# v of four pairs computed at once and kept in memory, and six merge gates moved into the pairs of a three-branch decoder layer

## The chip, the cores and the metric

The kernel runs on one core of a Trainium2 chip. The metric is the device time of one execution in microseconds. Before the change it is 1905.27 us, the median of three runs (1904.55 to 1906.85).

## What is computed

One layer on a sequence of S = 1024 rows of width D = 1024, all in float32. The input is normalised to h, and one projection of h with 14 blocks of columns feeds three branches; a convolution with a layer norm (a), a gated linear recurrence over 8 heads of 128 (b), and attention with a forget gate over 16 heads of 64 (c). Each branch is multiplied by its own gate, projected, weighted by a merge gate and summed; the sum is projected once more and added to the input. Cut to what matters here:

```python
h = rms_norm(x, g)
p = h @ w_in                              # columns: a: val, glu, gate; b: q, f, i, gate; c: q, k, v, gate, f; merge
out_b = hgrn2(silu(q), f, i, lb, g)       # v = i: scores @ v, state += k^T v, per head of 128
logits = q @ k.T / 8 + F[:, None] - F[None, :]   # c: F = cumsum(log_sigmoid(f))
out_c = softmax(causal(logits)) @ v
y = sum(sigmoid(merge[b]) * ((branch[b] * silu(gate[b])) @ w_branch[b]) for b in "abc")
out = x + y @ w_out
```

For `scores @ v` both branches need v with the sequence in the partitions: 8 blocks of 128 rows by 128 columns for each head of b, and the same for each two heads of c.

## The kernel before

**Projections.** A job is a product of 128 columns of a weight matrix with the whole sequence. Each float32 factor is split into a high and a low part (`whi`, `wlo` by `split` at L342, ScalarE casts, VectorE subtracts; `hT_hi`, `hT_lo` for h), and three products are added up: hi by hi, hi by lo, lo by hi. So a job is 2 halves (512 columns of the sequence each) of 8 x 3 = 24 matmuls of 128x512, with the weights stationary. The result has the projected columns in the partitions and the sequence in the free dimension. Three of the eight PSUM banks take turns for these jobs (`ps_lin`, L224); the other five are for the attention and the recurrence.

**Order of the jobs.** `lin` (L359) goes through the list `jobs` that is built from L1141 on. First stands the narrow job of the forget gate of c (`fgate_done`, L411, with a scan over the sequence and 8 small transposes in `fgate2`, L435). Then come 8 pairs; a pair c holds q, k, v, gate of two heads of branch c (`col(7)` to `col(10)`) and q, f, v, gate of one head of branch b (`col(3)` to `col(6)`), 8 jobs in all. After the pairs stand the convolution's jobs, the branch projections of c and b (`bjob`) with the merge gates of c, b, then the gate of a (`ag`), the eight merge gates of a (`mjob("a", j)`), the eight projections of a and the output.

**v.** The two v jobs of a pair write v into a tile `vT` (columns in the partitions); `vprep` (L549) then turns it with 8 transposes of 128x128 on TensorE into two PSUM banks, and ScalarE copies these into the tile `V`. The attention (`att`, L579) or the recurrence (`hgrn`, L711) of the pair starts at the end of this.

**What sets the order of the work.** While the program is written, a planner (`Sched`, L86) runs `lin` and the coroutines of attention, recurrence and convolution side by side, by its own estimates of each engine's time, and so decides how their instructions are mixed. 18 work tiles of 128x1024 (`F`, class `Free`, names fa0 to fa9 and fb0 to fb7) go round among all of them. Each engine then executes its instructions in the order in which they are written, and a wait holds up all that stands behind it on its engine. All DMAs are issued from one queue, SP's, in order too. The fb tiles are given up after the last pair (`swap`, L1157), and the branch inputs `yhi`, `ylo` take their memory; `yload` (L960) then reads the first of them.

**The end of the pairs.** The recurrence of a head ends with a partition all-reduce on GpSimd, a logarithm and an exponential with a table load each on ScalarE, a product on VectorE, and a store into `yb`.

Of the kernel before, what the change touches and what calls it, by code (L numbers as in the profile page):

```python
# [39 lines left out]
ORD = "01ab"  # L40
AHB = 2
# [8 lines left out]
class Free:  # L50
# [148 lines left out]
def build(tc, x, norm_g, w_in, conv_w, conv_b, ln_g, ln_b, hgrn_g, f_bias, qn_g, kn_g,  # L199
# [93 lines left out]
    mdram = dram.tile([KT, P, S], F32, name="mdram")  # L293

# [42 lines left out]

    def fetch(j):
# [20 lines left out]
    def lin(jobs, hooks):  # L359
        seq = [(0, 0), (1, 0), (2, 0), (0, 1), (1, 1), (2, 1)]  # L360
        seq += [(n, h) for n in range(3, len(jobs)) for h in (0, 1)]
        for m, (n, half) in enumerate(seq):
            j = jobs[n]
            for i in {3: (3,), 5: (4,)}.get(m, (n + 2,) if n > 2 and not half else ()):
                if i < len(jobs):
                    fetch(jobs[i])
            for i in {5: (3,)}.get(m, (n + 1,) if n > 2 and not half else ()):
                if i < len(jobs):
                    split(jobs[i])
# [166 lines left out]
    def v_pre(st):  # L536
        def f():
            yield need(2 + RES)
            st["vT"], st["V"] = F.get(), F.get()
        return f  # L540

    def v_done(st, tag, cb):
        def f(half, hs, ps):
            sc.act(st["vT"][:, hs], ps, AF.Copy)
            if half == 1:
                sc.start(vprep(st, tag, cb), f"v{tag}{st['c']}")
        return f

    def vprep(st, tag, cb):  # L549
        vT, V = st["vT"], st["V"]  # L550
        yield
        pss = yield from bget(2)
# [4 lines left out]
        bput(*pss)  # L557
        yield
        fput(vT)
        st["v"] = True  # L560
        if cb is not None:
            cb()

    def g_pre(st):
        def f():
            yield need(1 + RES)
            st["gt"] = F.get()
# [417 lines left out]
    def br_pre(b, j):  # L985
        def f():
            if b != "c":
# [150 lines left out]
    def col(o, c, w=P):  # L1138
# [4 lines left out]
                    narrow=True))  # L1143
    t128 = [const.tile([P, KT], F32, name=f"t128_{i}") for i in range(2)]
    for c in range(KT):
# [4 lines left out]
        jobs.append(Job(col(9, c), hX, v_done(sa, "c", (lambda s: lambda: sc.start(att(s), f"att{s['c']}"))(sa)), v_pre(sa)))  # L1150
        jobs.append(Job(col(10, c), hX, g_done(sa), g_pre(sa)))
        jobs.append(Job(col(3, c), hX, bq_done(sb), bq_pre(sb)))
        jobs.append(Job(col(4, c), hX, bf_done(sb), bf_pre(sb)))
# [192 lines left out]
```

## Time and profile before

| | before |
|---|---|
| median of three runs | 1905.27 us (1904.55 to 1906.85) |
| profiled execution, its own time | 1904.65 us |
| span of its trace | 1902.9 us |
| TensorE busy | 1885.2 us, 99% |
| VectorE busy | 1285.2 us, 68% |
| ScalarE busy | 953.6 us, 50% |
| GpSimd busy | 186.2 us, 10% |
| DMA moved | 140.82 MB, mean 74 GB/s |

The busy shares are means over unlike stages. In the pairs (about 55 to 1000 us) ScalarE is busy 74% of the time and VectorE 68%; in the stage of the convolution (1110 to 1450 us) VectorE is busy 96%, ScalarE 17%; in the last stage (from 1548 us) both are mostly idle. TensorE has next to no gap in any of them, at a granted clock of 1.00 but for one stretch in the first 40 us. The durations of single matmuls overlap (0.39 us each, 0.23 us from start to start), so lengths of time on TensorE are read from starts.

### The profile page before, as it was taken

To read this page: it belongs to the slowest core of one execution; us is meant where nothing else is said; L and a number is where in the kernel's file an instruction comes from. 1 tells how busy PE (TensorE), PEld (TensorE's weight loads), DVE (VectorE), ACT (ScalarE), POOL (GpSimd) and SP (SyncE) were. 2 spreads that over 40 slices of the span, in tenths; PEclk is the share of its full clock that TensorE was granted. 3 is DMA by queue.
4 is the path that set the end of the run, shared out by engine and by line. 5 is a ranking of instruction groups with operands and counts; after the bars stand their busy time and mean duration, and the time that the engine had idled before them with its cause. 6 is when DMAs were issued, how large, how long until landed. Compare 5 with 4: busy or idle time off the path is not lost.

```text
span 1902.9 us, 27032 instructions
## 1 busy us (share of the span) xinstructions
PE 1885.2 (99%) x11075; PEld 1548.8 (81%) x11075; DVE 1285.2 (68%) x1692; ACT 953.6 (50%) x1508; POOL 186.2 (10%) x164
## 2 busy tenths in 40 slices
PE   8999999999999999999999999999999999999999
PEld 6877878878878788787887888888888888888888
DVE  6567595775856857659577999999995467413431
ACT  6777768767687687776875411111221234321210
POOL 2021120211202111112021100000000010000000
PEclk9999999999999999999999999999999999999999
DMA  4111101111111111110111322222444553213431
GB/s 147 48 31 45 56 23 45 56 45 45 34 45 45 34 52 38 45 56 23 45 56 46 133 78 67 78 67 67 134 147 151 194 160 92 85 45 104 118 129 49
DMA packets 173011, 140.82 MB, mean 74 GB/s; under 512 B 4909, under 2 KB 155445, under 8 KB 172888
## 3 DMA queue, kind: packets, MB, share of 16 engines
q1 hardware_dynamic: 172888, 139.10, 23.7%
q8 instruction: 86, 1.41, 0.3%
q14 instruction: 37, 0.30, 0.1%
HBM read 109.72 MB, written 29.36 MB: 73 GB/s over the span
## 4 chain that ended last, share of the span: by engine, by line
PE 85%; ACT 7%; DVE 3%; DMA 3%; issue 1%; SPq 0%; POOL 0%; DVEq 0%; ACTq 0%; POOLq 0%
PE bank L111 84%; ACT fb L124 4%; ACT khi L124 1%; DVE fa L128 1%; PE bank L115 1%; ACT L124 1%; DMA zdram<-fa 1%; ACT fa L124 1%; DVE fb L128 1%; DMA fa<-zdram 1%; DMA fb<-in_hgrn_norm_g_dram 1%; DMA wraw<-in_w_in_dram 0%; ACT whi L354 0%; DVE klo L132 0%; DVE wlo L355 0%
## 5 line engine op out<-in xcount | busy, mean ns | idle before, releaser
L111 PE MATMUL bank<-hT_hi,whi 128*128 128x512 f32 x1792 | 706.8, 394 | 0.0
L111 PE MATMUL bank<-hT_hi,wlo 128*128 128x512 f32 x1792 | 701.3, 391 | 0.8 <-DVE wlo L355 0.8
L111 PE MATMUL bank<-hT_lo,whi 128*128 128x512 f32 x1792 | 701.2, 391 | 0.0
L111 PEld LDWEIGHTS bank<-hT_hi,wlo 128*128 128x128 f32 x1792 | 336.8, 188 | 72.9 <-issue 2.4
L111 PEld LDWEIGHTS bank<-hT_hi,whi 128*128 128x128 f32 x1792 | 337.0, 188 | 69.8 <-issue 3.2
L111 PEld LDWEIGHTS bank<-hT_lo,whi 128*128 128x128 f32 x1792 | 337.3, 188 | 63.8 <-issue 0.2
L354 ACT ACTIVATE whi<-wraw 128x1024 fp32r<-128x1024 f32 x137 | 144.9, 1058 | 356.9 <-PE bank L111 346.9
L132 DVE SCALAR_TENSOR_TENSOR fa<-fa,taps,fa 128x1024 f32<-128x1024 f32 x240 | 300.0, 1304 | 0.4
L355 DVE TENSOR_TENSOR wlo<-wraw,whi 128x1024 fp32r<-128x1024 f32 x137 | 191.8, 1400 | 112.2 <-ACT whi L354 109.9
L128 DVE TENSOR_TENSOR fa<-fa,fa 128x512 f32<-128x512 f32 (+3 forms) x226 | 173.8, 784 | 67.0 <-ACT fa L124 50.4
L124 ACT ACTIVATE fa<-bank 128x512 f32<-128x512 f32 (+2 forms) x182 | 102.5, 572 | 141.7 <-PE bank L111 131.0
L111 PE MATMUL bank<-yhi,whi 128*128 128x512 f32 x384 | 149.4, 389 | 0.0
L111 PE MATMUL bank<-yhi,wlo 128*128 128x512 f32 x384 | 149.2, 389 | 0.0
L111 PE MATMUL bank<-ylo,whi 128*128 128x512 f32 x384 | 149.2, 389 | 0.0
L124 ACT ACTIVATE fb<-bank 128x512 f32<-128x512 f32 (+5 forms) x262 | 114.2, 451 | 40.6 <-PE bank L111 32.1
L128 DVE TENSOR_TENSOR fa<-fa,fb 128x512 f32<-128x512 f32 (+1 forms) x121 | 81.8, 676 | 59.0 <-ACT fb L124 37.8
L124 ACT ACTIVATE fb<-bank,negF,rk 128x256 f32<-128x256 f32 (+1 forms) x184 | 89.2, 549 | 47.7 <-PE bank L111 31.8
L124 ACT ACT_TABLE_LOAD x83 | 106.5, 1283 | 4.5 <-DVE fb L128 3.0
L132 DVE SCALAR_TENSOR_TENSOR fa<-fa,bank 128x512 f32<-128x512 f32 x96 | 65.7, 686 | 60.0 <-PE bank L111 60.0
L124 ACT ACTIVATE fa<-fa 128x256 f32<-128x256 f32 (+3 forms) x109 | 75.9, 721 | 55.3 <-DMA zdram<-fa 29.6
L124 ACT ACTIVATE fb<-fb 128x1024 f32<-128x1024 f32 (+2 forms) x96 | 88.1, 953 | 15.8 <-DVE fb L128 14.8
L111 PEld LDWEIGHTS bank<-yhi,wlo 128*128 128x128 f32 x384 | 72.1, 188 | 15.0
(163 smaller groups left out, 2128.7 us busy)
## 6 DMA issues: line engine op xcount, KB each, us to landing
wraw<-in_w_in_dram SPq DMA_DIRECT2D x113, 512.0 KB, 3.8
wraw<-in_w_branch_dram SPq DMA_DIRECT2D x24, 512.0 KB, 3.9
zdram<-fa SPq DMA_DIRECT2D x16, 512.0 KB, 4.1
mdram<-fa SPq DMA_DIRECT2D x32, 256.0 KB, 2.0
fa<-mdram SPq DMA_DIRECT2D x16, 512.0 KB, 3.8
fa<-zdram SPq DMA_DIRECT2D x16, 512.0 KB, 3.3
fa<-in_x_dram SPq DMA_DIRECT2D x9, 512.0 KB, 5.2
yc<-fb SPq DMA_DIRECT2D x8, 512.0 KB, 2.6
```

What stands on the lines that cost most here:

```text
L111: self.nc.tensor.matmul(out, lhsT=lhsT, rhs=rhs, start=start, stop=stop)
L115: self.nc.tensor.transpose(out, in_, ident)
L124: return self.nc.scalar.activation(out, in_, func, **kw)
L128: self.nc.vector.tensor_tensor(out=out, in0=a, in1=b, op=op)
L132: self.nc.vector.scalar_tensor_tensor(out=out, in0=a, scalar=s, in1=b, op0=op0, op1=op1)
L354: pin(nc.scalar.activation(j.hi, j.raw, AF.Copy))
L355: pin(eng.tensor_tensor(out=j.lo, in0=j.raw, in1=j.hi.bitcast(F32), op=ALU.subtract))
```

## The change

For v, four pairs are done at once. A `VJob` takes 512 columns of v's weights (four pairs of one branch). Its weights stay in 8 of the work tiles, four for the high and four for the low parts (`vfetch`), and now slices of hT of 128 rows are stationary and the weights move: 8 groups of 24 matmuls of 128x512, each with a result of 128 rows of the sequence by 512 columns of v (`vgroup`). The result is copied to a work tile and stored to DRAM (`vdram`); `g_pre` of each pair reads the pair's 128 columns back into `V`. `vprep` with its transposes and copies is gone. The number of 128x512 matmuls is the same: 4 x 192 instead of 16 x 48. All four VJobs stand in pair 0: after k, after the gate of c, after q of b and after f of b.

The six merge gates of a with j = 2 to 7 are no longer computed after `ag`, but one each in pairs 1 to 6, behind the gate of c (`pjob`). Their tanh is stored to `gdram` and read back in `br_pre`. What each engine gets more or less, counted in the instructions of both kernels: TensorE 128 transposes less; ScalarE 32 copies of 128x512 less and 10 table loads more (84 to 94); VectorE as many as before; 60 more DMAs on SP's queue. In TensorE's order the kind of matmul changes (projection to something else or back) 327 times instead of 295.

The core of the diff:

```diff
+EARLY = [("a", j) for j in range(2, 8)]
...
+    vdram = {(t, h): dram.tile([4, P, S], F32, name=f"v{t}{h}") for t in "cb" for h in range(2)}
+    gdram = {(b, j): dram.tile([P, S], F32, name=f"g{b}{j}") for b, j in EARLY}
...
+    def vfetch(j):
+        yield need(KT + 2)
+        j.lo = [F.get(dt=F32R, w=S) for _ in range(4)]
+        j.hi = [F.get(dt=F32R, w=S) for _ in range(4)]
+        for n, (lo, hi) in enumerate(zip(j.lo, j.hi)):
+            raw = F.get()
+            nc.sync.dma_start(out=raw[:, 0:S].rearrange("p (k c) -> p k c", k=2),
+                              in_=j.src[n * 256:(n + 1) * 256].rearrange("(k p) c -> p k c", p=P))
+            with tc.high_priority(HP):
+                nc.scalar.activation(hi[:, 0:S], raw[:, 0:S], AF.Copy)
+                nc.vector.tensor_tensor(out=lo[:, 0:S], in0=raw[:, 0:S],
+                                        in1=hi[:, 0:S].bitcast(F32), op=ALU.subtract)
+            fput(raw)
...
+    def vgroup(j):
+        w = lambda ts, k: ts[k // 2][:, k % 2 * H2:(k % 2 + 1) * H2]
+        for i in range(KT):
...
+            ps = ps_lin()
+            for k in range(KT):
+                hh, hl = (h[:, k, i * P:(i + 1) * P] for h in hT)
+                sc.mm(ps, hh, w(j.hi, k), k == 0, False, 228)
+                sc.mm(ps, hh, w(j.lo, k), False, False, 228)
+                sc.mm(ps, hl, w(j.hi, k), False, k == KT - 1, 228)
...
+            sc.act(ot[:, i % 2 * H2:(i % 2 + 1) * H2], ps, AF.Copy)
+            if i % 2:
+                for n in range(2):
+                    nc.sync.dma_start(
+                        out=vdram[j.tag, j.half][:, :, (i - 1 + n) * P:(i + n) * P].rearrange("c p e -> p c e"),
+                        in_=ot[:, n * H2:(n + 1) * H2].rearrange("p (c e) -> p c e", c=4))
...
-    def vprep(st, tag, cb):
...
-        for k in range(KT):
-            sc.tr(pss[k // 4][:, k % 4 * P:(k % 4 + 1) * P], vT[:, k * P:(k + 1) * P], ident)
-        for half in range(2):
-            sc.act(V[:, half * H2:(half + 1) * H2], pss[half], AF.Copy)
...
-    def g_pre(st):
+    def g_pre(st, tag, cb):
...
+            nc.sync.dma_start(out=st["V"][:, 0:S], in_=vdram[tag, c // 4][c % 4])
...
+            if (b, j) in gdram:
+                yield need(1, True)
+                mg[b, j] = F.get(True)
+                nc.sync.dma_start(out=mg[b, j][:, 0:S], in_=gdram[b, j])
...
+        if c == 0:
+            jobs.append(VJob(col(9, 0, 4 * P), "c", 0))
...
+        elif early:
+            jobs += [pjob(*bj) for bj in early[:1]]
...
-    jobs += [mjob("a", j) for j in range(KT)]
+    jobs += [mjob("a", j) for j in range(KT) if ("a", j) not in gdram]
```

**VectorE at the start.** The rows of x are normalised one block of 128 after the other (`fa4`, `fa5`, the last are fa6 and fa7) and go to TensorE to be turned into hT; `vecs` is a table of small vectors that comes from TensorE. Before:

```order
L1246 TENSOR_SCALAR fa4_5_149<-fa4_5_149,ss_120 128x1024 [waits DMAHW6_49,DVE_49]
L1234 TENSOR_SCALAR ss_120<-ss_120 128x1 [waits Activation_49]
L1242 RECIPROCAL ss_120<-ss_120 128x1
L1243 SCALAR_TENSOR_TENSOR ss_120<-ss_120 128x1 [waits DVE_49]
L1244 TENSOR_SCALAR ss_120<-ss_120 128x1 [waits DVE_49]
L1246 TENSOR_SCALAR fa5_6_150<-fa5_6_150,ss_120 128x1024 [waits DMAHW5_49,DVE_49]
```

With the change, where `fb0_19` is the low part of the first weights of v:

```order
L1311 TENSOR_SCALAR fa4_5_159<-fa4_5_159,ss_120 128x1024 [waits DMAHW6_49,DVE_49]
L1299 TENSOR_SCALAR ss_120<-ss_120 128x1 [waits Activation_49]
L359 TENSOR_TENSOR fb0_19_549<-fa2_27_557,fa8_23_553 128x1024 [waits DMAHW3_49,DMAHW2_49,DMAHW4_49,DMAHW1_49,DMAHW6_49,DMAHW0_49,PE_49]
L1307 RECIPROCAL ss_120<-ss_120 128x1
L1361 COPY vecs_110<-bank7_83 128x280
L129 TENSOR_TENSOR fb4_13_370<-fb4_13_370,fb5_14_371 16x512 [waits Activation_49]
L1308 SCALAR_TENSOR_TENSOR ss_120<-ss_120 128x1 [waits DVE_49]
L1362 TENSOR_SCALAR taps_111<-vecs_110 128x248 [waits DVE_49]
...
L1311 TENSOR_SCALAR fa5_6_160<-fa5_6_160,ss_120 128x1024 [waits DMAHW5_49,DVE_49]
```

The subtraction for v's weights, which waits for TensorE, stands ahead of the normalisation of fa5 and of the two that follow.

**TensorE behind k of pair 0.** `fb1_18` is the result of the forget gate's scan; its transposes are the 128x16 rows. Before, the v job of pair 0 (`whi_541`, `wlo_542`) fills the time up to them, 45 matmuls of 128x512 (from the first row here to the last but one):

```order
L111 MATMUL bank0_76<-hT_hi_143,whi_541 128x512 [waits Activation_49]
L111 MATMUL bank0_76<-hT_lo_144,whi_541 128x512
L115 MATMUL bank4_80<-ident_84,fb3_17_417 128x128 x2
L111 MATMUL bank1_77<-hT_hi_143,whi_541 128x512 [waits Activation_49]
L111 MATMUL bank0_76<-hT_hi_143,wlo_542 128x512 [waits DVE_49]
...
L111 MATMUL bank1_77<-hT_hi_143,wlo_542 128x512
L115 MATMUL bank3_79<-ident_84,fb1_18_506 128x16 [waits DVE_49]
```

With the change, where fa8, fa9, fa0, fa1 hold the high parts and fb0, fb4, fb5, fb2 the low parts of the first VJob's weights:

```order
L112 MATMUL bank0_76<-fa8_23_553,hT_hi_153 128x512 [waits Activation_49]
L112 MATMUL bank0_76<-fb0_19_549,hT_hi_153 128x512
...
L112 MATMUL bank1_77<-fa9_24_554,hT_hi_153 128x512
L116 MATMUL bank4_80<-ident_84,fb3_17_427 128x128 x4
L116 MATMUL bank3_79<-ident_84,fb1_18_514 128x16 [waits DVE_49]
L116 MATMUL bank3_79<-ident_84,fb1_18_514 128x16 x7
L112 MATMUL bank0_76<-fb4_20_550,hT_hi_153 128x512 [waits DVE_49]
```

There are 14 matmuls of the VJob ahead of the transposes that wait for the scan, and the next ones need fb4_20. That tile takes the place of the scan's input, as VectorE's order shows (`fb4_13` and `fb5_14` are the scan's inputs):

```order
L483 MEMSET fb5_14_371 16x1024 [waits DVE_49]
L133 SCALAR_TENSOR_TENSOR klo0_131<-bank2_78,gk_115,khi0_129 64x512 [waits Activation_49]
L485 SCALAR_TENSOR_TENSOR fb1_18_514<-fb5_14_371,fb4_13_370 16x1024 [waits DVE_49]
L359 TENSOR_TENSOR fb4_20_550<-fa3_28_561,fa9_24_554 128x1024 [waits DMAHW7_49,DVE_49]
L359 TENSOR_TENSOR fb5_21_551<-fa4_29_565,fa0_25_555 128x1024 [waits DMAHW2_49]
```

**VectorE at the end of pair 7.** `fa1_277` before and `fb7_332` after is the tile of the last head's result, `fa4_294` and `fa3_351` the factor that the exponential gives, `ylo0` the first input of the branch projection of c; the rows with `taps` are the convolution. Before:

```order
L132 SCALAR_TENSOR_TENSOR fa8_298_8801<-fa6_297_8800,taps_111,fa8_298_8801 128x1024
L128 TENSOR_TENSOR fa1_277_8304<-fa1_277_8304,fa4_294_8655 128x1024
L132 SCALAR_TENSOR_TENSOR fa0_301_9155<-fa9_300_9154,taps_111,fa0_301_9155 128x1024
L132 SCALAR_TENSOR_TENSOR fa8_298_8801<-fa6_297_8800,taps_111,fa8_298_8801 128x1024
L128 TENSOR_TENSOR ylo0_9121<-ylo0_9121,yhi0_9113 128x1024
L128 TENSOR_TENSOR ylo1_9122<-ylo1_9122,yhi1_9114 128x1024
```

With the change:

```order
L129 TENSOR_TENSOR fb7_332_8610<-fb7_332_8610,fa3_351_9073 128x1024 [waits Activation_49]
L133 SCALAR_TENSOR_TENSOR fa1_355_9404<-fa8_354_9403,taps_111,fa1_355_9404 128x1024 [waits DVE_49] x5
L129 TENSOR_TENSOR ylo0_9370<-ylo0_9370,yhi0_9362 128x1024 [waits DMAHW3_49,DMAHW5_49,DMAHW2_49,Activation_49]
L133 SCALAR_TENSOR_TENSOR fa1_355_9404<-fa8_354_9403,taps_111,fa1_355_9404 128x1024 [waits DVE_49]
L129 TENSOR_TENSOR ylo1_9371<-ylo1_9371,yhi1_9363 128x1024 [waits DMAHW4_49,Activation_49]
L133 SCALAR_TENSOR_TENSOR fa1_355_9404<-fa8_354_9403,taps_111,fa1_355_9404 128x1024 [waits DVE_49]
L129 TENSOR_TENSOR ylo2_9372<-ylo2_9372,yhi2_9364 128x1024 [waits DMAHW5_49,Activation_49]
L406 TENSOR_TENSOR wlo_9710<-wraw_9635,whi_9709 128x1024 [waits DMAHW7_49,PE_49,Activation_49]
```

The last result now stands in an fb tile, whose memory goes to `yhi` and `ylo`. On TensorE 223 rows lay between the last matmul of the last head and the first of the branch projection of c, nearly all of them 128x512; now there are 72, all of them 128x512:

```order
L112 MATMUL bank7_83<-fa9_350_9072,fa2_349_9071 128x128 [waits DVE_49]
L112 MATMUL bank1_77<-hT_hi_153,whi_9637 128x512 [waits Activation_49]
...
L112 MATMUL bank2_78<-hT_hi_153,whi_9573 128x512 [waits Activation_49]
...
L112 MATMUL bank0_76<-hT_hi_153,whi_9637 128x512 [waits Activation_49]
...
L112 MATMUL bank2_78<-yhi0_9362,whi_9709 128x512 [waits DMAHW2_49,DMAHW1_49,DMAHW5_49,DVE_49,DMAHW7_49,Activation_49,Pool_49]
L112 MATMUL bank2_78<-ylo0_9370,whi_9709 128x512 [waits DVE_49]
L112 MATMUL bank2_78<-yhi0_9362,wlo_9710 128x512 [waits DVE_49]
```

The second of the three jobs' halves waits for ScalarE to empty bank2 into a tile (`fa3_357`) that takes the place of `fa3_351`, the factor above.

## Rows read from the trace of the kernel before

**Rows 1.** Page: busy time of TensorE; the convolution's group on VectorE (busy, mean ns, idle).

```profile
PE 1885.2 (99%) x11075; PEld 1548.8 (81%) x11075; DVE 1285.2 (68%) x1692; ACT 953.6 (50%) x1508; POOL 186.2 (10%) x164
...
L132 DVE SCALAR_TENSOR_TENSOR fa<-fa,taps,fa 128x1024 f32<-128x1024 f32 x240 | 300.0, 1304 | 0.4
```

**Rows 2.** Waits of TensorE: line, releaser, us in total, times, longest.

```profile
PE bank L111 <- ACT fa L124: 1.8, 7, 0.3
...
PE bank L111 <- DVE wlo L355: 0.8, 1, 0.8
```

**Rows 3.** Windows: length, busy us of PE, PEld, DVE, ACT, POOL; clock, DMA.

```profile
247.70:371.40 123.70, 123.17 (x883) 99.91 (x881) 84.49 (x133) 92.07 (x156) 20.01 (x15) 1.00 0.15 43
...
120.00:125.00 5.00, 4.34 (x38) 2.61 (x37) 5.00 (x10) 4.99 (x7) 0.00 (x0) 1.00 0.00 0
```

**Rows 4.** Timeline of TensorE: start, us, engine, line, operation, count.

```profile
59.40 0.39 PE L111 MATMUL bank<-hT_lo,whi 128*128 128x512 f32 x1
59.63 0.39 PE L111 MATMUL bank<-hT_hi,wlo 128*128 128x512 f32 x1
...
66.56 1.25 PE L115 MATMUL bank<-ident,fb 128*128 128x128 f32 x10
67.57 0.47 PE L111 MATMUL bank<-hT_hi,whi 128*128 128x512 f32 x1
```

**Rows 5.** Source line of the transposes: ns min, median, max.

```profile
L115 PE MATMUL bank<-ident,fb x200: 207/272/328, 55.1 to 997.4; 128*128 128x128 f32 x96, 16*128 16x16 f32 x4
```

**Rows 6.** Timeline at the start, TensorE and VectorE.

```profile
27.06 0.65 PE L1294 MATMUL bank<-ident,fb 35*128 35x35 f32 x8 [1.10 <-DMA fb<-in_hgrn_norm_g_dram]
...
29.26 0.80 DVE L1246 TENSOR_SCALAR fa<-fa,ss 128x1024 f32<-128x1024 f32 x1
...
31.34 1.22 DVE L355 TENSOR_TENSOR wlo<-wraw,whi 128x1024 fp32r<-128x1024 f32 x1
...
32.61 0.79 PE L111 MATMUL bank<-hT_hi,wlo 128*128 128x512 f32 x1
```

**Rows 7.** Windows at the start, columns as in group 3.

```profile
30.00:32.00 2.00, 1.89 (x9) 1.42 (x10) 1.89 (x6) 0.01 (x1) 0.00 (x0) 0.63 0.00 0
32.00:34.00 2.00, 1.98 (x6) 1.34 (x5) 1.85 (x3) 2.00 (x4) 0.00 (x0) 0.51 0.11 24
```

**Rows 8.** Timeline of the forget gate's chain: logarithm, scan, transposes.

```profile
56.54 1.15 ACT L124 ACTIVATE fb<-fb,one_t 16x1024 f32<-16x1024 f32 x1
...
61.85 2.27 DVE L427 TENSOR_TENSOR_SCAN fb<-fb,fb 16x1024 f32<-16x1024 f32 x1
...
65.16 0.66 PE L115 MATMUL bank<-ident,fb 16*128 16x16 f32 x8
```

**Rows 9.** Timeline from the last head's end to the branch projection of c.

```profile
1060.80 0.39 PE L111 MATMUL bank<-fa,fa 128*128 128x128 f32 x2
...
1061.97 6.11 POOL L869 PARTITION_ALL_REDUCE fb<-fa  x1 [0.60 <-ACT fa L124]
...
1062.58 5.00 DVE L132 SCALAR_TENSOR_TENSOR fa<-fa,taps,fa 128x1024 f32<-128x1024 f32 x1
...
1071.59 3.69 SPq L964 DMA_DIRECT2D ylo<-yc  x8
...
1072.87 1.06 ACT L124 ACTIVATE fa<-fa 128x1024 f32<-128x1024 f32 x1
...
1078.04 2.47 SPq L873 DMA_DIRECT2D yb<-fa  x1
...
1080.32 2.36 DVE L128 TENSOR_TENSOR ylo<-ylo,yhi 128x1024 fp32r<-128x1024 f32 x2
...
1094.18 1.23 DVE L128 TENSOR_TENSOR ylo<-ylo,yhi 128x1024 fp32r<-128x1024 f32 x1
...
1111.58 0.39 PE L111 MATMUL bank<-yhi,whi 128*128 128x512 f32 x1
```

**Rows 10.** Timeline of TensorE where the gate of a begins.

```profile
1548.16 0.50 PE L111 MATMUL bank<-hT_hi,wlo 128*128 128x512 f32 x1 [0.76 <-DVE wlo L355]
```

More of the change, by code (lines that the diff above doesn't have):

```diff
@@ L336, in __init__ @@
             self.raw = self.hi = self.lo = None
+    class VJob:
+        pre, narrow = None, False
+        def __init__(self, src, tag, half):
+            self.src, self.tag, self.half = src, tag, half
+    def vfetch(j):
[11 more added lines that the diff above has]
+            fput(raw)
+        sc.t["act"] += 4 * 950
+        sc.t["dve"] += 4 * 1240
+    def vgroup(j):
+        w = lambda ts, k: ts[k // 2][:, k % 2 * H2:(k % 2 + 1) * H2]
+        for i in range(KT):
+            if i % 2 == 0:
+                yield need(1)
+                ot = F.get()
+            ps = ps_lin()
[4 more added lines that the diff above has]
+                sc.mm(ps, hl, w(j.hi, k), False, k == KT - 1, 228)
+                if k == 3:
+                    yield 0
+            sc.act(ot[:, i % 2 * H2:(i % 2 + 1) * H2], ps, AF.Copy)
[4 more added lines that the diff above has]
+                        in_=ot[:, n * H2:(n + 1) * H2].rearrange("p (c e) -> p c e", c=4))
+                fput(ot)
+            yield 0
+        fput(*j.lo, *j.hi)
     def fetch(j):
@@ L364, in lin @@
             for i in {3: (3,), 5: (4,)}.get(m, (n + 2,) if n > 2 and not half else ()):
-                if i < len(jobs):
+                if i < len(jobs) and not isinstance(jobs[i], VJob):
                     fetch(jobs[i])
@@ L368, in lin @@
                 if i < len(jobs):
-                    split(jobs[i])
+                    if isinstance(jobs[i], VJob):
+                        yield from vfetch(jobs[i])
+                    else:
+                        split(jobs[i])
+            if isinstance(j, VJob):
+                if not half:
+                    yield from vgroup(j)
+                continue
             if not half and j.pre is not None:
@@ L1143, in build, with mcol, pjob, pre @@
                     narrow=True))
+    def mcol(b, j):
+        o = 11 * S + 16 + "abc".index(b) * S + j * P
+        return w_in[:, o:o + P]
+    def pjob(b, j):
+        st = {}
+        def pre():
+            yield need(1 + RES)
+            st["t"] = F.get()
+        def done(half, hs, ps):
+            sc.act(st["t"][:, hs], ps, AF.Tanh, scale=0.5)
+            if half == 1:
+                nc.sync.dma_start(out=gdram[b, j], in_=st["t"][:, 0:S])
+                fput(st["t"])
+        return Job(mcol(b, j), hX, done, pre)
     t128 = [const.tile([P, KT], F32, name=f"t128_{i}") for i in range(2)]
+    early = list(EARLY)
     for c in range(KT):
@@ L1170, in conv_jobs @@
         return [Job(col(1, c), hX, glu_done(s), glu_pre(s)), Job(col(0, c), hX, val_done(s))]
-    def mcol(b, j):
-        o = 11 * S + 16 + "abc".index(b) * S + j * P
-        return w_in[:, o:o + P]
     def mjob(b, j):
@@ L1193, in build @@
         jobs.append(bjob("b", j))
-        if j + AHB < KT:
+        if j + AHB < KT and ("b", j + AHB) not in gdram:
             jobs.append(mjob("b", j + AHB))
```

41 lines of the change are left out of this document (15 added, 26 removed).

## The prediction

> **What bounds the kernel now.** I read the page's busy times first: TensorE works 1885.2 of 1902.9 us, VectorE and ScalarE far less [rows 1]. So almost every microsecond that leaves TensorE's stream leaves the time, and every wait that enters it is paid in full. Next I read the list of TensorE's waits: nothing in it is above 2.5 us, and the two rows shown stand for the rest, seven short waits for ScalarE and one for VectorE [rows 2]. Then the windows: a pair is 123.7 us long with 123.17 on TensorE, 92.07 on ScalarE and 84.49 on VectorE, so these have 30 us of room there; only pair 0 has gaps, as 0.66 us in 120 to 125 [rows 3]. The chains that come close to TensorE are looked up in the timeline: the rows at the start [rows 6], the forget gate's scan [rows 8], the end of pair 7 [rows 9] and the start of the gate of a [rows 10]. What decides is whether the new order still hides these chains.
>
> The sum is made against the profiled execution, 1904.65 us (span 1902.9 and 1.75 us around it), which is 0.6 us under the median.
>
> **What is removed.** 128 transposes. Ten of them in a row take from 66.56 to 67.57, 0.101 us each from start to start [rows 4]: 128 x 0.101 = 12.9 us. They lie on the path, since TensorE has no gap. A projection matmul stands for 0.227 us (59.40 to 59.63), and the one behind transposes lasts 0.47 instead of 0.39 us [rows 4]: a change of kind costs 0.08 us. The new order has 32 more of these changes: 32 x 0.08 = +2.6; since the changes differ in kind I take +2 (0 to +3). The 32 copies on ScalarE had room and bring nothing by themselves. The projection's matmuls are as many as before at the same size: 0, with either operand stationary, since both kinds load 128 columns per 512 moving ones.
>
> The transposes' own durations are longer than their pitch, 272 ns in the median [rows 5], and 128 x 0.272 would be 34.8 us. The Trainium skill ("TensorE: Matmul & The Clock Gate", Part 4: PE-mode transpose) gives about 275 ns for one in a kernel. The trace agrees with that as the duration of one, but the next one starts after 101 ns. By the page's price the sum below would end 22.3 us lower, at 1894; the measured pitch decides.
>
> **The start.** Before, VectorE does the last three row blocks of x (one at 29.26) and then the low part of k's weights at 31.34, for which TensorE waits until 32.61 [rows 6]. Now the subtraction for v's weights stands ahead of three row blocks and waits for the small transposes that start at 27.06 and last 0.65 [rows 6]. The first of the three was done before 27 us in the kernel before. Going down the new order with these durations (subtraction 1.22, row block 0.80, some 0.5 of small ones for each), k's low part is ready near 34.7 to 35.1 instead of 32.56: +2.5 us (1 to 5; the casts of v's weights ahead of ScalarE's square roots, which wait for a DMA, make the upper end).
>
> **The first v group.** TensorE reaches it at the same place as before, 54.84. The new order has 14 matmuls (3.2 us) and 4 transposes, to about 58.6, and then the forget gate's transposes, which wait for the scan; the scan ends at 61.85 + 2.27 = 64.12 [rows 8]. Before, 45 matmuls filled that time. Behind the scan VectorE has to make the low part fb4_20, 1.22 us, in the scan's own tile, so TensorE goes on at about 65.7 to 66: some 7 us lost, of which 0.7 are transposes that it does meanwhile. I take +7 (5 to 9). Nothing else can fill in, because TensorE executes in order. The chain itself has no reason to end earlier: it begins with the logarithm at 56.54 [rows 8], behind the same narrow job.
>
> A gap of this length also costs clock. At the start TensorE was busy for only 1.68 of the 4 us from 26 to 30, and the granted clock was 0.63 and 0.51 in the next two windows [rows 7], between its levels of 2.4 and 1.2 GHz; matmuls were then 0.4 instead of 0.23 us apart. Those 4 us gave about 1.7 us less work than at 1.00 (0.37 x 2 + 0.49 x 2). One such price for the two long gaps together is +1.5 (0 to 3.4): a gap of 0.76 us left the clock alone [rows 10].
>
> **The rest of pair 0.** The later VJobs follow g, bq and bf, each of 10.9 us, in which their casts can run. Pair 0's own gaps of about 1 us partly go, and new ones of the same kind come in: -1 (-2 to +3).
>
> **Pairs 1 to 7.** A pair has 123.7 - 16 x 0.101 - 2 x 10.9 + 10.9 = 111 us of TensorE work with a gate, 100 without, and 88 to 89 us of ScalarE work (92.07 [rows 3] less four copies, more for the gate and table loads): 80% and in pair 7 88% instead of 74%. Waits for ScalarE like the seven of 0.3 us [rows 2] will be more: +1 (0 to 5). The reads of V from memory are issued a job or more ahead: 0. The gates' work is the same, moved: 0.
>
> **The end of pair 7.** Before, the last matmul of the last head is at 1060.80 and the branch projection of c begins at 1111.58, 50.8 us later; between them lie the all-reduce (1.2 us later, 6.11 long), two table loads and the exponential until 1073.93, the loads of ylo at 1071.59, and VectorE's low parts from 1080.32 until 1095.41 [rows 9], 35 us after the head's end. All of that is hidden. Now 72 matmuls, 16.3 us, are left to hide it. Counted from the last head's matmul: the first of the three job halves waits for ScalarE, behind two squares of 0.6: 1.4 us. The second needs bank2 emptied into the tile of the exponential's factor, and so waits for the all-reduce (to 7.3), logarithm, table load and exponential (to about 11) and VectorE's product (1.2): it starts at 13 instead of 6.8, 6 us lost. Then VectorE has five convolution steps at 1.3 [rows 1], the low parts at 1.18 each [rows 9] with steps between them, and the split of c's first weights: that is ready at 26 where TensorE is at 24.4, and the fourth to sixth low parts come about 0.5 to 1 us late each. Sum 1.4 + 6 + 1.6 + 2.2 = +11 (5 to 15). The store into yb, which stood behind the loads of ylo at 1078.04 [rows 9], now must land before the first of them because of the shared memory; at 2.47 us that is still under VectorE's time. VectorE's step beside the all-reduce takes 5.00 instead of 1.30 us [rows 9], which hits the steps ahead of the product here and makes the upper end.
>
> **The end.** Of the eight late gates two remain, 21.8 us, between the gate of a and its projection. What they covered, the last low part of branch a, needs about 8 us: 0. VectorE's layer norm ends 0.76 us behind TensorE at 1548.16 [rows 10] as before, because the convolution keeps its place among the jobs: 0 (0 to 3).
>
> **Sum:** -12.9 + 2 + 2.5 + 7 + 1.5 - 1 + 1 + 11 = +11.1, so 1915.8 profiled, 1916.4 as a median. I say 1916.
>
> **Rivals.** *The new waits are hidden after all (faster).* The orders list waits, not times: if VectorE's and ScalarE's chains at the first v group and at the end of pair 7 had ended when TensorE gets there, only the start and the changes of kind would be left of the losses: -12.9 + 2 + 2.5 = -8.4, 1896. For it: the same chains have room now, 50.8 against 35 us. Against: for the scan it would need 5.5 us of earlier work in a chain that starts with the narrow job. Chance 0.12. *The transposes at their duration (faster):* 1894, chance 0.06; the pitch speaks against it. *Half of it (no change):* the end of pair 7 is hidden, because the factor's tile or the all-reduce come earlier than I count, but the scan is not: +0.1, 1905; or the scan is and the end isn't: 1908. Chance 0.2. *ScalarE becomes the bound in the pairs (slower still):* at 80 to 88% busy, with chains through it, each pair loses 1 to 2 us where four table loads of 1.28 us or a VJob's copies come at the wrong time: +8 to +12 more, about 1926. For it: pair 0 at nearly full ScalarE and VectorE had the gaps of 120 to 125 [rows 3]. Chance 0.1. *The change doesn't do what it says:* V's read waits for its store behind something slow in SP's queue, and attention starts late; one 3 to 5 us landing exposed in each of 16 reads is +50 to +80. The stores are all issued in pair 0, so only its first reads are near: chance 0.02.
>
> **Chances.** The forecast, 1909 to 1923, has 0.5. The range that holds 8 in 10 takes the even case and the nearer part of the hidden one, and the nearer part of ScalarE's: 1896 to 1924. Faster by over 0.2% (3.8 us, about what a measurement of this kernel can tell from no change): 0.18; within 0.2%: 0.2; slower: 0.62.
>
> **What would show it.** In the trace of after: TensorE idle from about 58.6 to 65 with VectorE's scan as releaser, the granted clock below 1.00 behind it; k's second half of the start 2 to 3 us later; a wait of some 6 us of a projection for ScalarE behind the exponential at the end of pair 7, with the branch projection of c beginning about 25 us after the last head's matmul; pairs of 111 us, the last of 100. Wrong would be pairs with over 1 us idle each, a wait on V's or w's DMA, or the wait at the gate of a growing above 1 us.

## The result and the profile after

The changed kernel takes 1978.28 us (median, 1976.65 to 1979.45) against 1906.06 us on the same chip: ratio 1.038, 95% interval 1.037 to 1.0395. Slower was forecast, but 1916 with an upper end of 1924: the sign was right, the size was not. The profiled execution of after is 1976.65 us (span 1974.9), 72.0 us above that of before.

The page of after, its busy times and TensorE's granted clock in 40 slices, to be held against [rows 1]:

```profile
PE 1906.4 (97%) x10947; PEld 1543.7 (78%) x10947; DVE 1275.7 (65%) x1692; ACT 954.7 (48%) x1486; POOL 187.9 (10%) x164
...
PEclk8899999999999999999999999999999999999999
```

128 matmuls fewer (the transposes), and TensorE is "busy" 21 us longer. Work that was not added cannot make it so; a lower clock can. TensorE's waits (line, releaser, us in total, times, longest), where before, behind the kernel's first instructions, no entry came above 2.0 us in total (two of them in [rows 2]):

```profile
PE bank L112 <- DVE fb L133: 10.8, 8, 2.3
PE bank L116 <- ACT fb L125: 10.1, 6, 2.0
PE bank L112 <- DVE gt L129: 8.1, 4, 2.0
PE bank L112 <- ACT fa L125: 6.9, 3, 5.4
PE bank L1314 <- DVE fa L1311: 6.4, 3, 5.5
PE bank L116 <- DVE fb L485: 6.3, 1, 6.3
```

The windows cut the changed kernel at the end of k's job in pair 0 (62.68), at the all-reduces that end pair 0 and pair 7, and at the branch projection of c (1246); 120 and 1473 are points between (length, busy us of PE, PEld, DVE, ACT, POOL, clock, DMA):

```profile
0.00:62.68 62.68, 47.99 (x235) 39.25 (x236) 35.17 (x84) 39.71 (x66) 9.72 (x36) 0.89 0.51 160
62.68:120.00 57.32, 50.83 (x217) 41.13 (x216) 22.58 (x25) 27.70 (x36) 0.00 (x0) 0.91 0.24 71
120.00:363.37 243.37, 243.37 (x1394) 196.88 (x1393) 82.09 (x133) 101.91 (x172) 12.72 (x14) 1.00 0.23 67
363.37:1221.89 858.52, 823.54 (x5810) 650.35 (x5808) 606.25 (x941) 618.32 (x1020) 145.70 (x106) 0.98 0.17 53
1221.89:1246.00 24.11, 18.26 (x72) 14.71 (x73) 23.16 (x18) 12.14 (x14) 6.11 (x1) 0.93 0.50 194
1246.00:1473.00 227.00, 225.00 (x987) 184.47 (x987) 221.31 (x199) 36.39 (x45) 0.62 (x5) 1.00 0.24 75
1473.00:1974.90 501.90, 497.39 (x2240) 416.89 (x2238) 285.16 (x297) 118.48 (x138) 13.06 (x2) 1.00 0.41 132
```

The same marks of before, where pair 0 and the pairs stand in one window:

```profile
0.00:55.21 55.21, 47.71 (x240) 39.37 (x240) 32.74 (x82) 36.98 (x63) 9.74 (x36) 0.97 0.44 137
55.21:1060.80 1005.59, 1000.52 (x7102) 811.49 (x7101) 692.67 (x1072) 731.31 (x1226) 156.50 (x119) 1.00 0.15 43
1060.80:1111.58 50.78, 50.78 (x226) 42.10 (x225) 50.02 (x43) 20.61 (x24) 6.24 (x2) 1.00 0.42 142
```

From these (length less PE busy is idle time; of busy time that fell into stretches at the lower clock level half is counted as lost, an estimate):

| stage | forecast | idle, after | lost by the clock, after | both, before | difference |
|---|---|---|---|---|---|
| start, to the end of k in pair 0 | +2.5 | 14.7 | 3.3 | 9.2 | +8.8 |
| first v group and scan, with the clock of both long gaps | +8.5 | 6.5 | 3.4 | 0 | +9.9 |
| rest of pair 0, pairs 1 to 7 | 0 | 35.0 | 13.1 | 5.1 | +43.0 |
| end of pair 7 | +11 | 5.8 | 1.7 | 0 | +7.5 |
| after that | 0 | 6.5 | 0 | 5.1 | +1.4 |
| transposes | -12.9 | | | | -12.9 (priced by an experiment below) |
| not in idle time or clock | +2 | | | | +14.3 (what is left to 72.0) |

The pairs are the surprise: 43 us where I had put nothing. There TensorE idles in many short waits. Single ones from pair 4's timeline (start, us, engine, line, operation; in brackets the idle time before it and its releaser):

```profile
788.79 1.03 PE L112 MATMUL bank<-fb,fb 128*64 128x256 f32 x8
789.75 0.29 PE L112 MATMUL bank<-gt,fb 128*32 128x48 f32 x6
789.97 0.87 PE L112 MATMUL bank<-fa,fb 128*64 128x256 f32 x8
790.77 0.63 PE L112 MATMUL bank<-gt,fb 128*32 128x48 f32 x38
793.41 1.51 PE L112 MATMUL bank<-gt,fa 128*32 128x48 f32 x64 [2.02 <-DVE gt L129]
794.85 0.80 PE L112 MATMUL bank<-hT_hi,whi 128*128 128x512 f32 x1
```

Steps of attention (128x256) and of the recurrence (`gt`, 128x48) stand here with no projection matmul between them, and the last of them waits for VectorE, whose rows from 787.91 to 794 have no gap. Around the wait of 2.02 us the clock goes down: behind it projection matmuls start 0.42 to 0.60 us apart. Some 35 us later it is ScalarE:

```profile
826.05 0.40 PE L112 MATMUL bank<-hT_hi,whi 128*128 128x512 f32 x1
828.43 0.66 PE L116 MATMUL bank<-ident,fb 128*128 128x128 f32 x4 [1.98 <-ACT fb L125]
```

```profile
824.66 1.38 ACT L125 ACTIVATE khi<-bank,gk 64x512 fp32r<-64x512 f32 x2
826.07 1.69 ACT L125 ACTIVATE fa<-sd 32x256 f32<-32x256 f32 x4
827.78 0.60 ACT L125 ACTIVATE fb<-bank 128x512 f32<-128x512 f32 x1
```

The copy that the transposes need stands on ScalarE behind k's two copies and four of the recurrence; seven projection matmuls on TensorE (824.59 to 826.45) were not enough to cover them. ScalarE is busy 91 of this pair's 123 us: it is not the bound, it is late at this place. The pair as a whole (columns as above):

```profile
731.41:854.67 123.26, 116.60 (x814) 91.88 (x813) 82.78 (x134) 91.24 (x149) 20.95 (x15) 0.96 0.17 52
```

The same step in the trace of before waited 0.28 us:

```profile
679.35 0.66 PE L115 MATMUL bank<-ident,fb 128*128 128x128 f32 x4 [0.28 <-ACT fb L124]
```

### The profile page after: what moved, and what is told of

The parts are those of the page before. It is cut to its first block, busy times and chain, and to the rows that moved or that the text cites. A ratio compares the mean times of both kernels' runs of the same rounds, so it can differ in the third digit from the quotient of the medians.

```text
span 1974.9 us, 26918 instructions
## 1 busy us (share of the span) xinstructions
PE 1906.4 (97%) x10947; PEld 1543.7 (78%) x10947; DVE 1275.7 (65%) x1692; ACT 954.7 (48%) x1486; POOL 187.9 (10%) x164
## 5 line engine op out<-in xcount | busy, mean ns | idle before, releaser
L112 PE MATMUL bank<-hT_hi,whi 128*128 128x512 f32 x1536 | 611.7, 398 | 7.9 <-ACT fa L125 6.6
L112 PE MATMUL bank<-hT_lo,whi 128*128 128x512 f32 x1536 | 607.3, 395 | 0.0
L112 PE MATMUL bank<-hT_hi,wlo 128*128 128x512 f32 x1536 | 605.0, 394 | 0.1
L129 DVE TENSOR_TENSOR fa<-fa,fa 128x512 f32<-128x512 f32 (+2 forms) x311 | 237.2, 788 | 101.9 <-ACT fa L125 46.0
L125 ACT ACTIVATE fa<-bank 128x512 f32<-128x512 f32 (+6 forms) x227 | 105.8, 472 | 210.5 <-PE bank L112 190.3
L112 PE MATMUL bank<-fb,hT_hi 128*128 128x512 f32 x448 | 146.6, 396 | 0.2 <-DVE fb L359 0.2
L125 ACT ACTIVATE fa<-bank,negF,rk 128x256 f32<-128x256 f32 x200 | 95.0, 552 | 34.1 <-PE bank L112 32.9
L125 ACT ACTIVATE fa<-fa 128x1024 f32<-128x1024 f32 (+4 forms) x99 | 82.3, 842 | 42.8 <-DMA zdram<-fa 27.8
L112 PEld LDWEIGHTS bank<-fb,hT_hi 128*128 128x128 f32 x448 | 84.3, 189 | 19.3 <-issue 0.4
L112 PEld LDWEIGHTS bank<-ylo,whi 128*128 128x128 f32 x384 | 72.1, 188 | 16.8 <-DVE ylo L129 2.0
```

Of the source, the lines that this page charges most:

```text
L112: self.nc.tensor.matmul(out, lhsT=lhsT, rhs=rhs, start=start, stop=stop)
L125: return self.nc.scalar.activation(out, in_, func, **kw)
L129: self.nc.vector.tensor_tensor(out=out, in0=a, in1=b, op=op)
```

## Experiments

Theory A says that the pairs wait because too little projection work is left between the steps of attention and recurrence. B blames the moved gates, C the new place of attention and recurrence in the order, D the work tile that V holds. Ratios are to the kernel before, on the same chip.

**The gates alone.** The kernel before, and `pjob` with `gdram` from the change:

```diff
+        if c and early:
+            jobs += [pjob(*bj) for bj in early[:1]]
+            del early[0]
...
-    jobs += [mjob("a", j) for j in range(KT)]
+    jobs += [mjob("a", j) for j in range(KT) if ("a", j) not in gdram]
```

> The kernel before with the six gates moved into pairs 1 to 6; v as before, with its transposes. Theory A (cover): a pair's own chains of VectorE, ScalarE and GpSimd need about 119 us, and TensorE must have that much work in a pair to hide them. With the gate a pair has 134.6 us of it, so nothing is exposed: 1905 +-4, and no wait above 1 us in the pairs. Theory B (the gate itself, its tanh and table loads, disturbs ScalarE's order): 6 to 8 us lost in each of six pairs, 1945. Theory C (attention and recurrence start at another place, because V no longer comes from transposes): gates leave it alone, 1905.

Measured: 1903.9 us against 1904.55, ratio 1.0 (0.9989 to 1.0011). No difference, and in 250 to 1000 us TensorE idles 0.25 us:

```profile
250.00:1000.00 750.00, 749.75 (x5262) 602.11 (x5261) 471.27 (x760) 538.46 (x894) 117.01 (x85) 1.00 0.16 47
```

B is out: in the kernel before, the gates cost nothing. The loss comes with v.

**v alone.** The changed kernel with `EARLY = []`.

> The changed kernel with all eight gates of a left at their old place, so pairs 1 to 7 have 100 us of TensorE work each. Theory A: pairs 1 to 6 keep their length of about 119 us with 11 us more of waits each, and the 65 us of gates come on top at the end: 2035 to 2045. Theory B: the waits in the pairs go, 1978 - 45 = 1933. Theory C: the waits stay as they are, 1978 +-8.

Measured: 1997.31, ratio 1.0487 (1.0457 to 1.0518). Worse than with the gates by 19 us, so the gates help the changed kernel; B and C do not give that. But A as I had put it falls too: pairs did not stay at 119 us, most went to 110 to 112, with 10 to 13 us of waits and clock loss each. There is no fixed length below which a pair can't go.

```profile
690.87:801.25 110.38, 101.51 (x768) 81.17 (x767) 80.78 (x132) 85.73 (x145) 23.62 (x17) 0.98 0.16 49
```

**Two gates per pair.** The changed kernel with twelve gates:

```diff
-EARLY = [("a", j) for j in range(2, 8)]
+EARLY = [(b, j) for j in range(2, 8) for b in "ba"]
...
-            jobs += [pjob(*bj) for bj in early[:1]]
-            del early[0]
+            jobs += [pjob(*bj) for bj in early[:2]]
+            del early[:2]
```

> The changed kernel with two gates in each of pairs 1 to 6 (j = 2 to 7 of a and of b), so these pairs have 122 us of TensorE work. Theory A: the chains are covered again, pairs of 122 to 123 us with under 1.5 us of waits each: 1978 - 65 + 6 x 3 = 1930. Theory B: waits double, over 2000. Theory C: waits as now, 1978 +-8.

Measured: 1964.02, ratio 1.0312 (1.0282 to 1.0342). The pairs came out as A says (123.84 us with 122.42 of TensorE, against 117.6 to 123.3 with 112 to 117 in the changed kernel), but not the sum: without the six gates of b the layer norm lost its cover, and TensorE waits for it in one piece.

```profile
1707.80 0.80 PE L112 MATMUL bank<-hT_hi,whi 128*128 128x512 f32 x1 [25.47 <-DVE fa L133]
```

**Each gate twice.** To add the cover and take it from nowhere:

```diff
-            jobs += [pjob(*bj) for bj in early[:1]]
+            jobs += [pjob(*bj) for bj in early[:1] * 2]
```

> The changed kernel with each of the six gates computed twice in its pair; nothing is taken from a later stage. TensorE gets 6 x 10.9 = 65 us more work. Theory A (cover: the pairs' chains need about 122 us of TensorE work to hide): the waits of the pairs go, and of the 65 us only some 15 to 25 are seen: 1993 to 2003. Theory C (the waits belong to the new places of attention and recurrence, whatever the cover): all 65 are seen, 2043.

Measured: 2004.91, ratio 1.0529 (1.0508 to 1.055): 65 us of work more, 26.6 us of time more than the changed kernel's 1978.28. Of TensorE's waits in pairs 2 to 6 one kind is left, ten of 0.7 us in the mean, and the clock stays up:

```profile
PE bank L112 <- ACT fb L125: 7.1, 10, 0.8
```

```profile
746.21:870.08 123.87, 122.45 (x866) 97.17 (x865) 82.97 (x133) 92.40 (x152) 19.80 (x15) 1.00 0.20 61
```

So 39 us of the 43 come back as soon as a pair has eight projection jobs again. This run and the next carry the verdict on the pairs.

**Less work in the old kernel.** The kernel before with the v jobs cut to the product hi by hi; v keeps its path, transposes and all:

```diff
-                sc.mm(ps, j.hi[:, k, :], a, k == 0, False, 228)
-                sc.mm(ps, j.hi[:, k, :], b, False, j.narrow and k == KT - 1, 228)
-                if not j.narrow:
+                sc.mm(ps, j.hi[:, k, :], a, k == 0, j.cut and k == KT - 1, 228)
+                if not j.cut:
+                    sc.mm(ps, j.hi[:, k, :], b, False, j.narrow and k == KT - 1, 228)
+                if not j.narrow and not j.cut:
...
+        jobs[-6].cut = jobs[-2].cut = True
```

> The kernel before, with the two products that hold a low part left out of the v jobs (16 matmuls of 128x512 each instead of 48), so v is only rounded; all else, the transposes too, as before. TensorE has 2 x 32 x 0.227 = 14.5 us less in every pair, 116 us in all, and a pair has some 109 us of its work, as after the change. Theory A (cover): pairs become 116 to 120 us long with waits of the same kinds as in the changed kernel, and only 30 to 60 us are gained: 1845 to 1875. Theory C (the waits come from v's new path): pairs of 109 us, 1905 - 116 + at most 10 = 1789 to 1800.

Measured: 1880.32, ratio 0.987 (0.9844 to 0.9895). 116 us of matmuls are gone and 25 us of time: even less than A had said. Pairs 1 to 6 are 118 to 122 us long, with waits for ScalarE and VectorE of the same kinds as in the changed kernel (columns as above; the two largest releasers in 200 to 1000 us are copies by ScalarE, 20.2 and 15.6 us):

```profile
682.52:801.49 118.97, 110.48 (x816) 87.90 (x815) 80.90 (x133) 91.62 (x154) 25.68 (x16) 0.99 0.16 45
```

Here v is neither moved nor read from memory, and attention starts where it always did. So v's new path is not needed for the waits, less projection work is enough, and A stands, as a rule of degree. Idle time and clock loss of a pair, against its work (busy time less the clock's part): 1.4 us with 122 (dup_gates, pairs 2 to 6), 3 to 11 with 109 to 116 (the changed kernel, pairs 2 to 6), 5 to 18 with 104 to 113 (v_cut, pairs 1 to 6), 10 to 13 with 92 to 102 (v_only, pairs 1 to 6). Pairs of like work still differ by several us, so the order in which the planner sets the steps counts too. No run changed that order alone; whether another order would cover the chains with seven jobs stays open.

**A later start of attention and recurrence.** In the changed kernel the call that starts them goes from `g_pre` to the end of the gate's first half:

```diff
-            st["v"] = True
-            cb()
+            st["v"], st["cb"] = True, cb
...
+            if half == 0:
+                st["cb"]()
```

> The changed kernel, but attention and recurrence of a pair are started by the planner after the first half of the gate's job, not before it; about where the transposes let them start before. Theory A: the chains only shift, 1978 +-8. Theory B: 1978 +-8. Theory C: the waits in the pairs go to the level of before, 1935.

Measured: 1984.76, ratio 1.0421 (1.0391 to 1.0451), 6 us above the changed kernel. As the cause of the whole loss C is out. The place does move the waits: idle time and clock loss fall in pairs 4 to 6 (4.0 to 4.7 us each, 6.8 to 11.2 in the changed kernel) and rise in pairs 1 to 3 (11 to 17 us, 3 to 9 there).

**V read later.** In the changed kernel `g_pre` takes one tile, and V is read at the beginning of `att` and `hgrn`:

```diff
-            yield need(2 + RES)
-            st["gt"], st["V"] = F.get(), F.get()
+            yield need(1 + RES)
+            st["gt"] = F.get()
...
+            def vget():
...
+        yield from st["vget"]()
```

`vget` takes the tile and issues the DMA from `vdram`; `att` and `hgrn` call it.

> The changed kernel, but V is read back, and takes its work tile, at the beginning of attention or recurrence, not ahead of the gate's job. Theory D (the pairs wait because g_pre needs eight free tiles before a projection may go on): the projections come in earlier, the waits in the pairs fall by half or more, 1950 to 1960. Theory A: the amount of work decides, not the tile, 1978 +-8.

With the changed kernel again on the same chip as base:

> The changed kernel once more, as the base for the next two on the same chip: 1978 +-3 by every theory.

Measured: 1961.96 (ratio 1.0298, 1.0277 to 1.0319) against 1979.08 (1.0386, 1.0369 to 1.0404): 17 us gained, which is nearer to D's 1950 to 1960 than to A's 1978 +-8. The pairs that it was read from keep their 119 us (696.80 to 815.53 and 815.53 to 934.88), so the tile is not what makes a pair long, but it has a part: idle time and clock loss of pairs 1 to 7 fall from 50 us (after_again) to 36, short of D's half. Behind pair 7 they fall from 15 to 8, since the wait there is gone.

**The two losses at the start.** q of b in front of the first VJob (f and the gate of b move ahead too, so that every VJob stands one job later), and the first VJob's casts and subtractions held in program order with x's row blocks:

```diff
+                pin = K if (j.tag, j.half) == ("c", 0) else (lambda ins: ins)
+                pin(nc.scalar.activation(hi[:, 0:S], raw[:, 0:S], AF.Copy))
...
+        if c == 0:
+            jobs.append(Job(col(3, c), hX, bq_done(sb), bq_pre(sb)))
+            jobs.append(VJob(col(9, 0, 4 * P), "c", 0))
```

> The changed kernel with q of b in front of the first VJob in pair 0, and the first VJob's casts and subtractions held behind the row blocks of x on their engines. What it tests: the two losses at the start, which the traces put at 7.5 us (start) and 9.9 us (scan, with the clock). If these are separate losses, both go and the time is 1978 - 17 = 1961 +-4. If the pairs swallow it (they wait for chains that end at the same time anyway), 1970 to 1978.

Measured: 1965.37, ratio 1.0321 (1.03 to 1.0342): 12.9 us of the 17 gained. The start reads as before, and the scan is not waited for; 4 us of new waits stand behind the VJobs of pair 0, the longest this one:

```profile
203.88 1.74 PE L112 MATMUL bank<-fa,fa 128*64 128x256 f32 x16 [3.10 <-ACT fa L125]
```

**Filling the scan's wait.** In the changed kernel, 24 useless matmuls in `fgate2`:

```diff
+        for n in range(24):
+            nc.tensor.matmul(pt, lhsT=hT[0][:, n % 8, 0:P], rhs=hT[0][:, n % 8, 0:H2], start=True, stop=True)
```

> The changed kernel with 24 matmuls of 128x512 of no use in front of the forget gate's transposes, where TensorE stands still for 6.3 us; their result is overwritten. They take 5.4 us that were idle, so by themselves they change nothing. If the clock after the wait costs what the trace says (6.8 us of work at the low level, half of it lost), the granted clock stays up and 3.4 us are gained: 1974.9 against 1978.3. If the clock costs nothing there: 1978.

Measured: 1980.91 (1977.23 to 1982.78) against 1979.08 (1977.01 to 1981.42) without: no gain to be seen. Locally it did what it should: the wait for the scan is gone (1.24 us for the low part behind it are left), the granted clock stayed at 1.00 and the all-reduce that ends pair 0 came at 360.57 instead of 363.97 (after_again), the forecast 3.4 us. One pair later 1.0 of it is left (494.83 and 495.87), at the end of pair 7 nothing (1224.52 and 1224.09), as the pairs' waits and clock stretches fall out differently. A gain ahead of stages that wait can be lost in them, though of v_later's 17 us 12.9 arrived; and 3.4 us are no more than the spread of these runs.

**The price of the transposes.** The kernel before with each of v's transposes done twice:

```diff
-        for k in range(KT):
+        for k in [k for k in range(KT) for _ in range(2)]:
             sc.tr(pss[k // 4][:, k % 4 * P:(k % 4 + 1) * P], vT[:, k * P:(k + 1) * P], ident)
```

> The kernel before with each of the 128 transposes of v done twice, for their price alone. By their pitch of 0.101 us: +12.9, 1918. By their duration of 0.272 us: +34.8, 1940. If they stand where TensorE would wait anyway: 1905.

Measured: 1917.83 against 1904.2, ratio 1.0073 (1.0058 to 1.0088), or 11 to 17 us for 128 of them. The pitch of 0.101 us, which gives 12.9, is right, and 272 ns, which gives 34.8, is not.

**Versions that should win.** If the pairs need eight jobs, give them eight and take them from where they aren't needed. The gate of branch a (`ag`) is computed in the pairs, its product stored, and a coroutine does the rest behind the layer norm; the merge gates of a stay there as its cover:

```diff
...
+ADV = [("g", j) for j in range(8)] + [("b", j) for j in range(2, 6)]
+TAIL = [("b", j) for j in (6, 7)]
...
+            jobs += [adv(*bj) for bj in early[:2]]
...
-        jobs.append(Job(col(2, c), hX, ag_done(s), ag_pre(s)))
-    jobs += [mjob("a", j) for j in range(KT) if ("a", j) not in gdram]
+    jobs += [pjob("a", j) for j in range(KT)]
```

> v at once as in the changed kernel, with the start as in v_later, and with the work chosen so that the pairs stay covered and the layer norm too: two jobs are moved into each of pairs 1 to 6 (the eight gates of branch a itself, stored to memory, and the merge gates b 2 to 5), b 6 and 7 stand behind pair 7, and the eight merge gates of a stay behind the projections of b, where they hide the layer norm. Theory A: no long wait is left, and the transposes' 12.9 us are gained: 1892 to 1900. Theory C: the pairs wait as in the changed kernel, 1940 to 1950.

Measured: 1964.24, ratio 1.0319 (1.0302 to 1.0336). Pairs 3 to 6 are covered, but the inputs of a's projection come too late; five such waits, 21 us, and the clock with them:

```profile
1750.35 1.65 PE L114 MATMUL bank<-yhi,whi 128*128 128x512 f32 x3 [5.84 <-ACT yhi L127]
```

With twelve jobs moved, and the loads of that coroutine one step ahead:

> As the run covered, with twelve jobs moved instead of fourteen (the gate of branch a and the merge gates b 2 to 5, two in each of pairs 1 to 6; b 6 and 7 at their old place), and the inputs of branch a's last step loaded one step ahead. Theory A (work decides): waits of 1.5 us per pair, none at the projection of a, 1964 - 35 + 10 to 15 for pairs 0 to 2 that stay: 1925 to 1932; if the short waits go too, 1900. Theory D (the tile decides): the same, since its pairs are covered anyway.

Measured: 1971.16, ratio 1.0351 (1.0335 to 1.0366); the same waits, in 1750 to 1850 us 21 us idle and 8 lost by the clock, and at the end of pair 7 a wait of 6 us again. And with V read later on top:

> covered2 with V read back, and its tile taken, at the beginning of attention or recurrence. Theory D: pairs 0 to 2, where covered still waited some 19 us, lose their waits too, 1905 to 1912. Theory A: as covered2 within 4 us.

Measured: 1960.35, ratio 1.029 (1.0273 to 1.0307). Pairs 0 and 1 lose their long waits, as D said, but the time doesn't come near 1905. Of the 57 us by which its trace is longer than that of before, idle time and clock loss behind pair 7 make 30 (most of it at a's projection again), those up to there 23, and 4 are left over. No version of v at once that I tried beats the kernel before.

## Why the prediction was wrong

**Transposes, -12.9.** Right, by double_tr; but the waits in the pairs and the costlier starts (both below) take back more than that.

**Pairs 1 to 7, +1 (0 to 5).** This is the step that failed; the windows give +43 (with the rest of pair 0, for which I had -1). I took the room of ScalarE and VectorE from the window's means, 30 us of 123.7 [rows 3], and concluded that a pair of 111 us would still hide them. The means say that the engines have the time; they do not say that TensorE has something to do while each single step runs. A pair's projections are that something. The change took two of eight jobs out of a pair and put one in; dup_gates, which puts in a second, and v_cut, which takes 14.5 us of matmuls a pair from the old kernel, show that this is what the loss hangs on. Pairs with over 1 us idle each stand in the prediction as a sign of being wrong, and they came. My rival of ScalarE as the bound had the right place and sign, but was sized at 1 to 2 us per pair for a wrong reason: ScalarE is busy 74 to 76% of pairs 2 to 6, and waits for VectorE count at least as much.

**The clock, +1.5 (0 to 3.4).** Too low by far: 19.7 us more than before. I had counted two long gaps. In the pairs, waits of 2 us were followed by the lower level too: of the eleven waits of 1.9 to 2.4 us in pairs 1 to 7 seven, with 13.1 us lost, so nearly their own length again. Four of 1.98 to 2.02 us were not (before 828.43, 917.03, 1036.01 and 1069.77), and in the other profiled execution of the same kernel (after_again) it was partly others. So the length of a wait alone does not tell.

**Start, +2.5 (1 to 5).** +7.5 in length (62.68 against 55.21; 8.8 by idle time and clock). The order was read rightly, the wait behind it was not: ScalarE stands 7.33 us for the DMA of v's weights, with x's squares behind it; I had named that and kept it under 5.

```profile
28.27 1.06 ACT L358 ACTIVATE fa<-fa 128x1024 fp32r<-128x1024 f32 x1 [7.33 <-DMA fa<-in_w_in_dram]
```

```profile
32.06 1.11 PE L1314 MATMUL bank<-ident,fa 128*128 128x128 f32 x4 [5.49 <-DVE fa L1311]
36.56 1.12 PE L1314 MATMUL bank<-ident,fa 128*128 128x128 f32 x4 [3.38 <-DVE ss L1299]
40.48 0.79 PE L112 MATMUL bank<-hT_hi,wlo 128*128 128x512 f32 x1
```

The matmul that waited for k's low part until 32.61 [rows 6] now starts at 40.48.

**First v group, +7 and a share of the clock.** Right: 14 matmuls, four transposes, then the wait for the scan, and the clock at its lower level behind it (windows as above, and the rows that answer to [rows 8]):

```profile
72.73 1.03 PE L116 MATMUL bank<-ident,fb 16*128 16x16 f32 x8 [6.26 <-DVE fb L485]
73.99 0.80 PE L112 MATMUL bank<-fb,hT_hi 128*128 128x512 f32 x1 [0.23 <-DVE fb L359]
```

```profile
72.00:74.00 2.00, 1.04 (x9) 0.94 (x9) 1.97 (x3) 0.20 (x1) 0.00 (x0) 0.50 0.00 0
74.00:76.00 2.00, 2.00 (x5) 1.61 (x6) 1.94 (x3) 0.82 (x3) 0.00 (x0) 0.50 0.45 83
80.00:82.00 2.00, 2.00 (x10) 1.65 (x9) 0.00 (x0) 0.00 (x0) 0.00 (x0) 1.00 0.00 0
```

**End of pair 7, +11 (5 to 15).** Right in mechanism, 7.5 in size up to 1246, 1.7 of it clock, and 1.1 of waits behind that. The all-reduce, the exponential, VectorE's product, ScalarE emptying the bank, and TensorE's wait of 5.4 us (forecast 6) stand in the forecast order; behind them the low parts of c's inputs cost 0.7 in three waits instead of 2.2, and the split of c's first weights 0.4 instead of 1.6. The rows answer to [rows 9]:

```profile
1221.89 6.11 POOL L903 PARTITION_ALL_REDUCE fa<-fa  x1 [2.65 <-ACT fa L125]
...
1230.50 1.06 ACT L125 ACTIVATE fa<-fa 128x1024 f32<-128x1024 f32 x1
...
1231.59 1.23 DVE L129 TENSOR_TENSOR fb<-fb,fa 128x1024 f32<-128x1024 f32 x1
...
1232.85 1.09 ACT L125 ACTIVATE fa<-bank 128x512 f32<-128x512 f32 x2 [1.29 <-DVE fb L129]
...
1233.50 0.80 PE L112 MATMUL bank<-hT_hi,whi 128*128 128x512 f32 x1 [5.40 <-ACT fa L125]
```

**Changes of kind, +2 (0 to 3).** Some 14 us remain that are neither idle time nor clock nor transposes. In the traces the kind changes 518 times instead of 478, 40 more where the orders gave 32. A covered pair of dup_gates has eight jobs and 16 transposes less than one of before and is still 123.9 us long, not 122.1: 0.9 of that is idle time, the rest stands in starts that come a little late, with more changes of kind in TensorE's order (68 in that pair in the trace, 58 before). The starts say which changes cost: a projection matmul behind an attention step of 128*64 starts 0.31 us after it, where steps of that kind follow each other 0.10 apart in the mean; behind a step of 128*128 with 128x256 it starts 0.12 after it, as a step of the same kind does. The four steps here take 0.58 us up to the projection:

```profile
798.59 0.65 PE L112 MATMUL bank<-fa,ones 128*64 128x256 f32 x4
799.17 0.50 PE L112 MATMUL bank<-hT_hi,whi 128*128 128x512 f32 x1
```

The trace of before has 8 places of the costly kind, that of after 36: at about 0.2 us each some 5 of the 14, by estimate.

**The projection's matmuls, 0.** The VJobs' matmuls start 0.231 us apart, the others' 0.227 to 0.228: for 768 of them some 3 of the 14. No run tested either term, and the rest of the 14 is open.

**The end and the DMAs, 0.** Right: the gate of a, which begins at 1684.95, waits for nothing, no wait on a read of V or a gate is in the list, and gates_only shows that moving the gates is free where the pairs are full.

## What to carry to other kernels

Where one engine is full because two latency-bound chains are threaded between its independent work, that work is not only load but cover: before making it shorter or moving it, count for each step of the chains what stands beside it, and price the steps that lose their neighbour. Mean busy shares of the other engines did not show this here. A test that costs one run is to leave out the work in the old kernel and see how much of it is gained: here 25 of 116 us.

## What the runs showed of the hardware

TensorE's granted clock fell to its lower level not only behind long gaps: seven of eleven waits of about 2 us inside otherwise full stretches were followed by it (the 2.02 us before 793.41, with matmuls 0.43 instead of 0.23 us apart behind it). Four were not (the 1.98 us before 828.43), nor were 0.76 us in the kernel before [rows 10]:

```profile
793.41:797.11 3.70, 3.69 (x70) 3.17 (x71) 3.70 (x8) 1.12 (x3) 0.00 (x0) 0.58 0.00 0
828.43:832.13 3.70, 3.70 (x18) 3.13 (x19) 1.40 (x2) 3.65 (x7) 0.00 (x0) 1.00 0.00 0
```

And the trace's busy time hides this: TensorE's busy time rose by 21 us although 128 instructions were taken away. The Trainium skill ("TensorE: Matmul & The Clock Gate", Part 4: PE-mode transpose) gives about 275 ns for a bf16 transpose of 128x128 in a kernel. For the float32 ones of this kernel the trace has nearly that as the duration (272 ns in the median, [rows 5]), but doubling 128 of them cost 13.6 us, 0.106 each.
